# Softmax times V on one core: range checks on the chip and a second, conditional loop

## The chip, the core and the metric

The kernel runs on one core of a Trainium2 chip. The core has five engines with an instruction stream each: TensorE (PE, matrix products; loads of its stationary operand are listed as PEld), VectorE (DVE), ScalarE (ACT), GpSimd (POOL) and SyncE (SP, which here issues every DMA). Names with a q (SPq, PEldq, DVEq) stand for an engine's sequencer: register, branch, semaphore and DMA-issuing instructions, which the profile does not count as busy time. Tiles live in SBUF, results of PE in PSUM. The metric is the device time of the whole program in microseconds; before the change it is 1063.91 us, the median of three runs (1063.54 to 1064.08).

## The reference

Inputs are `scores` of shape 8 x 12 x 1024 x 1024 and `v` of shape 8 x 12 x 1024 x 64, both float32 and normally distributed.

```python
scores_max = np.max(scores, axis=-1, keepdims=True)
attn = np.exp(scores - scores_max)
attn = attn / (np.sum(attn, axis=-1, keepdims=True) + 1e-8)
return np.matmul(attn, v).astype(np.float32)
```

There are 96 heads (8 x 12). Scores are 403 MB, v and the output 25 MB each.

## The kernel before

The kernel takes exp of the scores without subtracting the row maximum, in fp16, and gets each row's sum as an extra column of the product: v is kept in fp16 with columns of ones behind its 64 columns (`vones`, D + 1 = 65 columns used), so that the 65th column of the result is the sum of the row's exponentials.

A loop on the chip (line 307) runs over the heads in steps of AHEAD = 4; one pass of the loop is called a pass here, and there are 24. Within a pass the four heads (k = 0 to 3) and the eight rows of each (r = 0 to 7; a "row" is a block of 128 query rows) are written out. A row goes through these steps:

- ACT takes exp of 128 x 1024 scores from `s_nat` to `p_nat` (line 266), two rows per instruction, single rows in the last head of a pass after its first pair.
- PE turns the row in eight 128 x 128 pieces into PSUM, `psT` (line 279).
- DVE copies `psT` to SBUF, `pt` (line 286).
- PE multiplies the eight pieces of `pt` with `vones` and accumulates 65 columns in a PSUM bank, `psO` (line 150). This runs three rows behind the transposes (LAG = 3); four rows share a bank.
- After four rows, `normalise` has DVE take the reciprocals of the four sums (line 128) into `recip` and multiply (line 134, two instructions) into `out_sb`.

Data is moved in large pieces. Scores come as 4 MB per head into one of four buffers `s_nat0` to `s_nat3` (line 202), v as 1 MB per four heads into the only buffer `v_sb` (line 214); POOL casts v into `vones` with four instructions per head (`spread_v`, line 223) when that head's products are done, for the pass after. The output goes back as 512 KB per two heads (line 175).

The order on SP is fixed by hand (`queue`): in a pass it is scores of head 0, scores of head 1, store of heads 0 and 1, and then, in conditional blocks at the end (`last`, lines 240 and 247), scores of head 2, v, scores of head 3, store of heads 2 and 3. Each is a wait for the buffer and then a DMA; the v load waits until POOL has cast the last head of the pass. The last two passes take other arms of these conditionals: the scores of the very last head come in pieces of 3, 2, 1, 1 and 1 rows, and the last pass loads nothing. The order of PE's instructions is fixed by `in_line`. DVE's order is left to the planner that schedules the loop body, but for the places where `after` pins an instruction behind another. At the end of the loop each engine compares and branches (line 307); at the end of the program SP waits for all that is under way, and the engines meet in three barriers (line 336).

Of the kernel before, what the change touches and what calls it, by code (L numbers as in the profile page):

```python
# [7 lines left out]

FP32 = mybir.dt.float32
FP16 = mybir.dt.float16  # L10
EXP = mybir.ActivationFunctionType.Exp


@with_exitstack
def kernel(
# [6 lines left out]
    nc = tc.nc  # L22
    P = 128

    B, H, SQ, SK = scores.shape
    Bv, Hv, SKv, D = v.shape
    assert (B, H, SK) == (Bv, Hv, SKv)
    BH = B * H
    assert SQ % P == 0 and SK % P == 0
    R = SQ // P  # L30
    C = SK // P
    M = D + 1
    EB = 2
    G = 4
    LAG = 3
    AHEAD = 4
    Q = P // AHEAD
    S = P // Q
    L = 4
    T = 2  # L40

# [3 lines left out]
    sc_bh = scores.rearrange("b h (p r) j -> (b h) p r j", p=P)  # L47
    v_bh = v.rearrange("b h (i t) d -> (b h i) (t d)", i=Q)


    W = P // T
    out_bh = out.rearrange("b h (j x) d -> (b h j) (x d)", j=W)

    const_pool = ctx.enter_context(tc.tile_pool(name="const", bufs=1))
    sb_pool = ctx.enter_context(tc.tile_pool(name="sbpool", bufs=1))
    ps_pool = ctx.enter_context(tc.tile_pool(name="pspool", bufs=1, space=bass.MemoryType.PSUM))

    ident32 = const_pool.tile([P, P], FP32, name="ident32")
    make_identity(nc, ident32)
    order16 = const_pool.tile([P, P], FP16, name="order16")  # L60

    nc.vector.tensor_copy(  # L62
        out=order16[:].rearrange("p (t j) -> p t j", t=T),
        in_=ident32[:].rearrange("p (j t) -> p t j", t=T),
    )


    vones_bufs = []
    for k in range(AHEAD):
        vo = const_pool.tile([P, C, D + 2], FP16, name=f"vones{k}")  # L70
        nc.vector.memset(vo[:, :, D : D + 2], 1.0)  # L71
# [4 lines left out]
    def buffers(pool, count, shape, dtype, name):  # L76
        return [pool.tile(shape, dtype, name=f"{name}{k}") for k in range(count)]

    s_bufs = buffers(sb_pool, AHEAD, [P, R, SK], FP32, "s_nat")
    v_sb = sb_pool.tile([P, C // L, S, L, D], FP32, name="v_sb")  # L80
    p_bufs = buffers(sb_pool, 8, [P, EB, SK], FP16, "p_nat")
    pt_bufs = buffers(sb_pool, 4, [P, SK], FP16, "pt")
    out_bufs = buffers(sb_pool, 2, [P, T, R, D], FP32, "out_sb")
    rc_bufs = buffers(sb_pool, 2, [P, R // G, G, 1], FP32, "recip")
    psT_bufs = buffers(ps_pool, 4, [P, SK], FP16, "psT")


    psO_bufs = buffers(ps_pool, 2 * (R // G), [P, 512], FP32, "psO")
    turn = {}

    def take(bufs):
        k = turn.get(id(bufs), 0)
        turn[id(bufs)] = k + 1
        return bufs[k % len(bufs)]
# [5 lines left out]
    def after(a, b):  # L100

        tc.add_manual_dep(
            a.ins,
            b.ins.name,
            mybir.DependencyInfo(mybir.DependencyClass.NoSync, mybir.DependencyReason.DATA),
            reason="order",
        )

    def in_line(op):

        if line:
            after(op, line[-1])
        line.append(op)

    def queue(dma):

        if queued:
            after(dma, queued[-1])
        queued.append(dma)

    def one(bh, n):
        return bh[bass.ds(n, 1)].rearrange("o p r d -> (o p) r d")

    def normalise(k, st, b, behind=None):

        psO = st["psO"][b][:, 0 : G * M].rearrange("p (g m) -> p g m", m=M)
        recip = st["recip"][:, b]
        inverse = nc.vector.reciprocal(out=recip, in_=psO[:, :, D : D + 1])  # L128
        if behind is not None:
            after(inverse, behind)  # L130
        h = k % T
        for t in range(T):
            part = slice(t * W, (t + 1) * W)
            nc.vector.tensor_tensor(  # L134
                out=st["out_sb"][h * W : (h + 1) * W, t, b * G : (b + 1) * G, :],
                in0=psO[part, :, 0:D],
                in1=recip[part].to_broadcast([W, G, D]),
                op=mybir.AluOpType.mult,
            )

    def finish(u):

        n0, k, r, pt, st = u
        b, g = r // G, r % G
        if r == 0:
            st["recip"] = take(rc_bufs)
            st["out_sb"] = out_bufs[k // T]
        bank = st["psO"][b]
        for c in range(C):
            product = nc.tensor.matmul(  # L150
                out=bank[:, g * M : (g + 1) * M],
                lhsT=pt[:, c * P : (c + 1) * P],
                rhs=st["vones"][:, c, 0:M],
                start=(c == 0),
                stop=(c == C - 1),
            )
            in_line(product)
        if g == G - 1 and (b > 0 or k < AHEAD - 1):
            normalise(k, st, b)
        if r == R - 1:  # L160
            spread_v(k)
            if k == T - 1:
                store(n0, 0)
# [35 lines left out]
    def load(k, n, parts=(R,), r=0, **cond):  # L199
        for rows in parts:  # L200
            queue(
                nc.sync.dma_start(  # L202
                    out=s_bufs[k][:, r : r + rows, :],
                    in_=one(sc_bh, n)[:, r : r + rows, :],
                    **cond,
                )
            )
            r += rows
# [11 lines left out]
    def spread_v(k):  # L220

        for s in range(S):
# [4 lines left out]
                in_=v_sb[k * Q : (k + 1) * Q, :, s],  # L227
            )

    def load_next(k, n0):  # L230

        if k < AHEAD - 2:
            load(k, (n0 + (AHEAD + k)) % BH, cond=n0 < BH - AHEAD)

    def last(n0):


        before = queued[-1:]

        with tc.If(n0 < BH - 2 * AHEAD) as cmp:  # L240
            queued[:] = before
            load(AHEAD - 2, (n0 + (2 * AHEAD - 2)) % BH)
            load_v((n0 + 2 * AHEAD) % BH)
            load(AHEAD - 1, (n0 + (2 * AHEAD - 1)) % BH)
            store(n0, AHEAD - T)
        with cmp.Else():
            with tc.If(n0 < BH - AHEAD) as cmp2:
                queued[:] = before
                load(AHEAD - 2, BH - 2, (4, 4))
                load(AHEAD - 1, BH - 1, (3,))  # L250
                store(n0, AHEAD - T)
                load(AHEAD - 1, BH - 1, (2, 1, 1, 1), 3)
            with cmp2.Else():
                queued[:] = before
                store(n0, AHEAD - T, whole=False)

    def heads(n0):

        for k in range(AHEAD):
            st = dict(vones=vones_bufs[k], psO=[take(psO_bufs) for b in range(R // G)])  # L260
            for r in range(R):
                if r % EB == 0:
                    p_nat = take(p_bufs)
                    rows = 1 if k == AHEAD - 1 and r > 0 else EB
                    for g in range(0, EB, rows):
                        exp = nc.scalar.activation(  # L266
                            out=p_nat[:, g : g + rows, :].rearrange(
                                "p r (x v) -> p x r v", v=Q * L
                            ),
                            in_=s_bufs[k][:, r + g : r + g + rows, :].rearrange(  # L270
                                "p r (i x l) -> p x (r i) l", i=Q, l=L
                            ),
                            func=EXP,
                        )
                        rewrite(p_nat, exp)
                p_row = p_nat[:, r % EB, :].rearrange("p (h q l) -> p h l q", q=P, l=L)
                psT = take(psT_bufs)
                for c in range(C):
                    turned = nc.tensor.transpose(  # L279
                        out=psT[:, c * P : (c + 1) * P],  # L280
                        in_=p_row[:, c // L, c % L, :],
                        identity=order16[:],
                    )
                    in_line(turned)
                pt = take(pt_bufs)
                copy = nc.vector.tensor_copy(out=pt[:], in_=psT[:])  # L286
                rewrite(pt, copy)
                if k == AHEAD - 1 and r == R - 1:

                    normalise(k, st, 0, copy)  # L290
                if r == R - 1:
                    load_next(k, n0)
                pending.append((n0, k, r, pt, st))
                if len(pending) > LAG:
                    finish(pending.pop(0))
        while pending:
            finish(pending.pop(0))
        last(n0)

    assert BH % AHEAD == 0 and BH >= 2 * AHEAD and SK == Q * S * C  # L300
    load_v(0)
    for k in range(AHEAD):
        load(k, k)
    for k in range(AHEAD):
        spread_v(k)
    load_v(AHEAD)
    with tc.For_i(0, BH, AHEAD, iteration_sync="reg_based") as n0:  # L307
        queued.clear()
        line.clear()
        heads(n0)  # L310


# [28 lines left out]
```

## Time and profile before

| | |
|---|---|
| median of three runs | 1063.91 us (1063.54 to 1064.08) |
| span of the profiled execution | 1061.94 us |
| last DVE instruction ends | 1057.94 us |
| last store issued, landed | 1058.36 us, 1060.23 us |
| bytes moved | 453.05 MB, mean 427 GB/s |
| exp, two rows (line 266) | 1901 ns, x312 |
| copy of a turned row (line 286) | 691 ns, x768 |
| reciprocal of 128 x 4 (line 128) | 174 ns, x192 |
| product of 64 x 256 (line 134) | 422 ns, x384 |
| cast of 32 x 512 (line 223) | 607 ns, x400 |

Times of single instructions are from the profile's table of groups; a mean is over all instructions of that line and shape. In a timeline, a line gives start, length, engine, source line, operation and count, and in brackets how long the engine had been idle before it and what ended that idle time. "Landing" of a DMA is when its last bytes are reported.

### The profile page before, as it was taken

How to read it: one execution, taken by the hardware profiler on the slowest of the kernel's cores; microseconds unless marked ns; L12 is line 12 of the kernel's file. 1: busy time of each engine (PE TensorE's matmuls, PEld its weight loads, DVE VectorE, ACT ScalarE, POOL GpSimd, SP SyncE). 2: the span in 40 equal slices, each digit the busy share in tenths (PEclk: the TensorE clock that was granted, in tenths of full speed). 3: DMA queues.
4: the chain of work that ended last, by engine and by line, in shares of the span. 5: the costliest groups of instructions: out<-in, count | busy, mean ns of one | idle time of the engine just before them, and what ended most of it. 6: DMA issues, size and time to landing. Idle time of an engine off the chain costs nothing.

```text
span 1061.9 us, 32592 instructions
## 1 busy us (share of the span) xinstructions
PE 723.4 (68%) x12288; PEld 688.6 (65%) x12288; DVE 702.2 (66%) x1349; ACT 740.1 (70%) x480; POOL 243.5 (23%) x406
## 2 busy tenths in 40 slices
PE   2766766667666777667586676867667676666776
PEld 2756766667666667666576675766566676666765
DVE  1766666757667666666676666766667576676767
ACT  3766776667767668676685866767666677666686
POOL 3122211131121311212112121122111311213113
PEclk9888888878888788887988778888888788898889
DMA  9999999999999999999999999999999999999996
GB/s 395 433 410 435 434 434 433 427 433 431 433 430 433 434 433 436 428 431 429 432 432 434 434 431 434 425 438 430 430 434 432 435 424 440 431 430 434 428 430 271
DMA packets 25332, 453.05 MB, mean 427 GB/s; under 512 B 2801, under 2 KB 3313, under 8 KB 9713
## 3 DMA queue, kind: packets, MB, share of 16 engines
q1 hardware_dynamic: 25328, 453.00, 99.4%
q8 instruction: 3, 0.05, 0.0%
q14 instruction: 1, 0.00, 0.0%
HBM read 436.21 MB, written 25.17 MB: 434 GB/s over the span
## 4 chain that ended last, share of the span: by engine, by line
DMA 61%; PE 14%; ACT 5%; PEld 5%; DVE 4%; POOL 3%; issue 3%; SPq 1%; POOLq 1%; ACTq 0%
DMA s_nat<-in_scores_dram 61%; PE psT L279 8%; PE psO L150 6%; ACT p_nat L266 5%; DVE pt L286 4%; POOL vones L223 3%; PEld L279 3%; PEld L150 2%; SPq L214 1%; SPq L202 0%; POOLq L223 0%; POOLq L240 0%; POOLq L307 0%; POOLq L336 0%; ACTq L266 0%
## 5 line engine op out<-in xcount | busy, mean ns | idle before, releaser
L266 ACT ACTIVATE p_nat<-s_nat 128x2048 f16<-128x2048 f32 (+1 forms) x456 | 709.3, 1630 | 219.1 <-DMA s_nat<-in_scores_dram 191.1
L279 PE MATMUL psT<-order,p_nat 128*128 128x128 f16 x6144 | 573.1, 250 | 314.3 <-ACT p_nat L266 313.8
L286 DVE COPY pt<-psT 128x1024 f16<-128x1024 f16 x768 | 520.4, 691 | 286.8 <-PE L150 102.5
L279 PEld LDWEIGHTS <-p_nat 128*128 128x128 f16 x6144 | 458.4, 125 | 341.3 <-ACT p_nat L266 340.9
L223 POOL CAST vones<-v_sb 32x512 f16<-32x512 f32 x400 | 242.8, 607 | 815.5 <-PE L279 442.8
L150 PE MATMUL psO<-vones,pt 128*128 128x65 f16 x6144 | 357.5, 205 | 18.4 <-DVE pt L286 17.7
L150 PEld LDWEIGHTS <-pt 128*128 128x128 f16 x6144 | 302.1, 107 | 26.0 <-DVE pt L286 25.1
L134 DVE TENSOR_TENSOR out_sb<-psO,recip 64x256 f32<-64x256 f32 x384 | 162.2, 422 | 62.3 <-DMA out_dram<-out_sb 50.3
L266 ACT ACT_TABLE_LOAD x24 | 30.8, 1283 | 94.3 <-PE psO L150 59.5
L128 DVE RECIPROCAL recip<-psO 128x4 f32<-128x4 f32 x192 | 33.4, 174 | 5.5 <-PE psO L150 5.5
L71 DVE MEMSET vones<- 128x16 f16 x4 | 0.2, 72 | 0.8 <-PEq L325 0.8
L62 DVE CAST order<-ident 128x128 f16<-128x128 f32 x1 | 0.2, 226 | 0.4 <-POOL ident masks.py:199 0.4
masks.py:199 POOL TENSOR_SCALAR_AFFINE_SELECT ident<-ident 128x128 f32<-128x128 f32 x1 | 0.3, 292 | 0.1
masks.py:197 POOL MEMSET ident<- 128x128 f32 x1 | 0.2, 204 | 0.3 <-POOLq L325 0.3
L325 POOL MEMSET const-float32-0.0<- 128x1 f32 x1 | 0.1, 98 | 0.3 <-issue 0.3
L325 POOL MEMSET const-bfloat16-1.0<- 128x1 bf16 x1 | 0.1, 100 | 0.0
L325 POOL MEMSET const-uint8-127<- 128x1 uint8 x1 | 0.1, 100 | 0.0
L325 POOL MEMSET const-float32-1.0<- 128x1 f32 x1 | 0.1, 98 | 0.0
## 6 DMA issues: line engine op xcount, KB each, us to landing
s_nat<-in_scores_dram SPq DMA_DIRECT2D x96, 4096.0 KB, 32.5
v_sb<-in_v_dram SPq DMA_DIRECT2D x24, 1024.0 KB, 18.6
out_dram<-out_sb SPq DMA_DIRECT2D x47, 512.0 KB, 26.2
s_nat<-in_scores_dram SPq DMA_DIRECT2D x2, 2048.0 KB, 31.4
s_nat<-in_scores_dram SPq DMA_DIRECT2D x1, 1536.0 KB, 32.2
s_nat<-in_scores_dram SPq DMA_DIRECT2D x3, 512.0 KB, 20.8
s_nat<-in_scores_dram SPq DMA_DIRECT2D x1, 1024.0 KB, 25.0
out_dram<-out_sb SPq DMA_DIRECT2D x1, 256.0 KB, 2.5
```

The source lines that it names most:

```text
L62: nc.vector.tensor_copy(out=order16[:].rearrange("p (t j) -> p t j", t=T), in_=ident32[:].rearrange("p (j t) -> p t j", t=T),)
L71: nc.vector.memset(vo[:, :, D : D + 2], 1.0)
L128: inverse = nc.vector.reciprocal(out=recip, in_=psO[:, :, D : D + 1])
L134: nc.vector.tensor_tensor(out=st["out_sb"][h * W : (h + 1) * W, t, b * G : (b + 1) * G, :], in0=psO[part, :, 0:D], in1=recip[part].to_broa ...
L150: product = nc.tensor.matmul(out=bank[:, g * M : (g + 1) * M], lhsT=pt[:, c * P : (c + 1) * P], rhs=st["vones"][:, c, 0:M], start=(c == 0) ...
L214: nc.sync.dma_start(out=v_sb[:].rearrange("x h s l d -> x (h s l d)"), in_=rows[bass.ds(n // AHEAD, 1)].rearrange("o x y -> (o x) y"),)
L223: nc.gpsimd.tensor_copy(out=vones_bufs[k][s * Q : (s + 1) * Q, :, 0:D].rearrange("i (h l) d -> i h l d", l=L), in_=v_sb[k * Q : (k + 1) * ...
L266: exp = nc.scalar.activation(out=p_nat[:, g : g + rows, :].rearrange("p r (x v) -> p x r v", v=Q * L), in_=s_bufs[k][:, r + g : r + g + ro ...
L279: turned = nc.tensor.transpose(out=psT[:, c * P : (c + 1) * P], in_=p_row[:, c // L, c % L, :], identity=order16[:],)
L286: copy = nc.vector.tensor_copy(out=pt[:], in_=psT[:])
L325: nc = _bacc.Bacc("TRN2", target_bir_lowering=False, num_devices=1)
```

## The change

Three things are added, and one is moved.

The reciprocals of the row sums are no longer written to two small buffers in turn, but to columns of one tile `seen` with 1 + 32 + 1 columns: one column for each of the 32 rows of a pass, one at the left for the smallest value seen so far, one at the right for the largest. At the end of each pass `spread_of(seen, 32)` brings both up to date with two reductions on DVE, and `judge` compares them with limits (sums between 1 and 60000), combines that with the verdict on v, and counts with a 128 x 1 matmul over the partitions how many of the 128 partitions are within the limits. DVE copies the count to an integer.

The sizes of v are watched: in each pass, after rows 3 and 7 of head 2 (k = AHEAD - 2), DVE takes the largest absolute value of two quarters of `v_sb` (128 x 512 each), and after row 7 brings the smallest and the largest of these up to date and compares them with limits (2^-6 to 60000). The same is done once before the loop for the first four heads' v.

After the loop all engines load the count and branch on it. If it is below 128, `general` computes all heads again in fp32 with the row maximum subtracted; the loop of it runs over the 96 heads one by one. The arm that falls through is the one without it.

```diff
-    rc_bufs = buffers(sb_pool, 2, [P, R // G, G, 1], FP32, "recip")
+    seen = const_pool.tile([P, 1 + AHEAD * R + 1], FP32, name="seen")
+    nc.vector.memset(seen, 1.0)
+    v_seen = const_pool.tile([P, 1 + VC + 1], FP32, name="v_seen")
+    nc.vector.memset(v_seen, 1.0)
...
     def normalise(k, st, b, behind=None):
...
-        recip = st["recip"][:, b]
+        at = 1 + k * R + b * G
+        recip = seen[:, at : at + G].rearrange("p (g o) -> p g o", o=1)
...
+    def spread_of(tile, n):
+
+        nc.vector.tensor_reduce(out=tile[:, 0:1], in_=tile[:, 0 : n + 1], axis=X, op=ALU.min)
+        nc.vector.tensor_reduce(
+            out=tile[:, n + 1 : n + 2], in_=tile[:, 1 : n + 2], axis=X, op=ALU.max
+        )
+
+    def watch_v(parts):
+        for i in parts:
+            flat = v_sb[:].rearrange("x h s l d -> x (h s l d)")
+            n = (C // L) * S * L * D // VC
+            nc.vector.tensor_reduce(
+                out=v_seen[:, 1 + i : 2 + i],
+                in_=flat[:, i * n : (i + 1) * n],
+                axis=X,
+                op=ALU.max,
+                apply_absolute_value=True,
+            )
+
+    def within(out, tile, n, low, high, also=None):
+        part = small("part")
+        if also is None:
+            nc.vector.tensor_scalar(
+                out=part, in0=tile[:, n + 1 : n + 2], scalar1=high, scalar2=None, op0=ALU.is_le
+            )
+        else:
+            nc.vector.scalar_tensor_tensor(
+                out=part, in0=tile[:, n + 1 : n + 2], scalar=high, in1=also,
+                op0=ALU.is_le, op1=ALU.mult,
+            )
+        nc.vector.scalar_tensor_tensor(
+            out=out, in0=tile[:, 0:1], scalar=low, in1=part, op0=ALU.is_ge, op1=ALU.mult
+        )
...
+    def judge(bank):
+
+        within(right, seen, AHEAD * R, 1.0 / SUM_MAX, 1.0, also=fits[:])
+        cell = bank[0:1, G * M : G * M + 1]
+        in_line(
+            nc.tensor.matmul(
+                out=cell, lhsT=right[:], rhs=vones_bufs[0][:, 0, D : D + 1], start=True, stop=True
+            )
+        )
+        nc.vector.tensor_copy(out=count[:], in_=cell)
+
+    def general():
+
+        s, x = s_bufs[0], s_bufs[1]
...
+        with tc.For_i(0, BH, 1) as n:
+            nc.sync.dma_start(out=s[:], in_=one(sc_bh, n))
...
+            for r in range(R):
+                nc.vector.tensor_reduce(out=lift, in_=s[:, r, :], axis=X, op=ALU.max, negate=True)
+                nc.scalar.activation(out=p_row, in_=s[:, r, :], func=EXP, bias=lift[:])
...
                 if k == AHEAD - 1 and r == R - 1:
 
                     normalise(k, st, 0, copy)
+                if k == AHEAD - 2 and r % G == G - 1:
+                    watch_v(range(r // G * VC // (R // G), (r // G + 1) * VC // (R // G)))
+                    if r == R - 1:
+                        spread_of(v_seen, VC)
+                        within(fits, v_seen, VC, V_MIN, V_MAX)
...
         while pending:
             finish(pending.pop(0))
+        spread_of(seen, AHEAD * R)
+        judge(st["psO"][-1])
         last(n0)
...
     for k in range(AHEAD):
         load(k, k)
+    watch_v(range(VC))
+    spread_of(v_seen, VC)
     for k in range(AHEAD):
         spread_v(k)
...
         heads(n0)
+
+    good = nc.values_load(count[:], min_val=0, max_val=P)
+    with tc.If(good < P, preferred_fallthrough_block=False):
+        general()
```

## The prediction

> **What bounds the kernel now.** I read the page first (busy shares, then the DMA queue's share), then the waits of the SP queue, then a timeline of one steady pass of the loop, then the last pass, where the steady state ends.
>
> ```profile
> span 1061.9 us, 32592 instructions
> PE 723.4 (68%) x12288; PEld 688.6 (65%) x12288; DVE 702.2 (66%) x1349; ACT 740.1 (70%) x480; POOL 243.5 (23%) x406
> ...
> q1 hardware_dynamic: 25328, 453.00, 99.4%
> ```
>
> No engine is over 70% busy, while the one queue that carries all data is busy for 99.4% of the span: the loop runs at the pace of the DMA. One steady pass (four heads) shows how much room is behind that; ACT's exponentials first, then what SP issues:
>
> ```profile
> 572.82 7.60 ACT L266 ACTIVATE p_nat<-s_nat 128x2048 f16<-128x2048 f32 x7 [4.78 <-DMA s_nat<-in_scores_dram]
> ...
> 604.38 7.31 ACT L266 ACTIVATE p_nat<-s_nat 128x2048 f16<-128x2048 f32 x4 [3.60 <-DMA s_nat<-in_scores_dram]
> 616.51 7.60 ACT L266 ACTIVATE p_nat<-s_nat 128x2048 f16<-128x2048 f32 x7 [4.82 <-DMA s_nat<-in_scores_dram]
> ```
> ```profile
> 570.19 0.34 SPq L202 DMA_DIRECT2D s_nat<-in_scores_dram  x1
> 587.96 0.33 SPq L214 DMA_DIRECT2D v_sb<-in_v_dram  x1
> 588.67 0.33 SPq L202 DMA_DIRECT2D s_nat<-in_scores_dram  x1
> ```
>
> ACT waits for scores; the period is 616.51 - 572.82 = 43.69 us. The latest issue is the pair at 587.96 and 588.67 (v, then head 3's scores), and what was queued ahead of it (the scores issued at 570.19) lands only at 604.38. So the pass can end some 604.4 - 588.7 = 15.7 us later before the DMA runs dry.
>
> The room ends with the last pass, which has no loads behind it. By stretches (start:end, length, busy us of PE, PEld, DVE, ACT, POOL, clock, DMA share), and DVE in order of time:
>
> ```profile
> 1024.70:1033.20 8.50, 7.48 (x119) 7.18 (x118) 6.43 (x11) 7.41 (x5) 0.00 (x0) 0.77 1.00 426
> 1033.20:1054.70 21.50, 18.68 (x374) 17.03 (x371) 19.86 (x39) 19.26 (x14) 7.27 (x12) 1.00 0.84 353
> ```
> ```profile
> 1043.40 0.69 DVE L286 COPY pt<-psT 128x1024 f16<-128x1024 f16 x1 [0.18 <-PE L279]
> 1044.13 0.88 DVE L134 TENSOR_TENSOR out_sb<-psO,recip 64x256 f32<-64x256 f32 x2
> 1045.04 1.94 DVE L286 COPY pt<-psT 128x1024 f16<-128x1024 f16 x3
> 1046.89 0.17 DVE L128 RECIPROCAL recip<-psO 128x4 f32<-128x4 f32 x1
> 1047.24 0.69 DVE L286 COPY pt<-psT 128x1024 f16<-128x1024 f16 x1 [0.18 <-PE L279]
> 1047.96 0.88 DVE L134 TENSOR_TENSOR out_sb<-psO,recip 64x256 f32<-64x256 f32 x2
> 1048.87 1.94 DVE L286 COPY pt<-psT 128x1024 f16<-128x1024 f16 x3
> 1050.73 0.17 DVE L128 RECIPROCAL recip<-psO 128x4 f32<-128x4 f32 x1
> 1051.08 0.69 DVE L286 COPY pt<-psT 128x1024 f16<-128x1024 f16 x1 [0.18 <-PE psT L279]
> 1051.80 0.87 DVE L134 TENSOR_TENSOR out_sb<-psO,recip 64x256 f32<-64x256 f32 x2
> 1052.71 1.94 DVE L286 COPY pt<-psT 128x1024 f16<-128x1024 f16 x3
> 1054.92 0.69 DVE L286 COPY pt<-psT 128x1024 f16<-128x1024 f16 x1 [0.27 <-PE L150]
> ```
>
> In the 21.5 us up to 1054.7 DVE is busy for 19.86 us, with idle bits of 0.18 us: it is the fullest engine, and its copies run 0.6 to 1.3 us behind the transposes that feed them (the last transposes end at 1054.25, their copy starts at 1054.92). Whatever DVE gets to do after 1033 moves the end.
>
> **The sum's base.** The profiled execution has a span of 1061.94 us; the median of the three runs is 1063.91, 1.97 us more, which I carry over. The measurement tells about 0.2% (2.1 us) from no change.
>
> **The change, part by part.**
>
> The reads of v (four reductions of 128x512 in head 2, after rows 3 and 7). No row has a reduction. The 128x4 reciprocal takes 174 ns and the 64x256 product 422 ns, 0.98 ns per element more; 512 elements come to 0.67 us. Bounds: 0.35 us, if it goes at the 0.65 us per 1024 of the f16 copies, and 0.69 us, a copy's whole time. I take 0.67 (it is f32, as the product is): 2.7 us a pass. Minimum, maximum and two comparisons of a few elements follow, each waiting for the one before: four times 0.174 + 0.035 (the gap from reciprocal to product at 1055.7), 0.84 us. Together 3.5 us of DVE per pass.
>
> In 23 passes that costs nothing: the cover is the 15.7 us. v lands in time, because it is queued right behind the scores of head 2: those land at 604.38, POOL's first cast of the new v starts at 606.89, and DVE copies row 3 of that head at 611.30. The v load now waits for DVE too, but it already waits for POOL's last cast of the pass, 10 us after head 2. Behind that wait on SP stand head 3's scores and a store, which is why the 15.7 us count.
>
> In the last pass the 3.5 us fall at 1044 and 1048, where DVE is behind. Of the idle bits after that (0.18, 0.18, 0.27) about 0.4 us can be filled. Cost 3.1 us. Bounds: 1.4 + 0.84 - 0.6 = 1.6 us and 2.8 + 0.84 = 3.6 us where the code's place holds; nothing, if the work comes where DVE idles (a rival).
>
> The judging at the end of each pass (minimum and maximum over 33 columns, two comparisons, a matmul, a copy to an integer). DVE needs about 4 x 0.21 = 0.85 us before PE may start, and PE's matmul stands ahead of the next pass's first transposes. In steady passes it is covered as above. At 1023 us, into the last pass, DVE's last product ends at 1023.0 and PE starts the new transposes at 1023.73; with the judging they start at about 1024.2. From there the chain has no wait for a load that takes it up: 0.45 us, from 0 to 0.8. After the last pass, judging takes 0.85 + 0.3 + 0.2 = 1.4 us from DVE's end at 1057.94, while the last store, issued at 1058.36, lands at 1060.23, and SP waits for that: nothing, with 0.9 us to spare.
>
> The branch at the end. All five engines load the count into a register, compare, branch, and meet again. I read the first of the closing barriers (1060.50 to 1060.93) as the loop's own, so this lies behind it, uncovered. Comparing and branching: the compare-branches take 0.05 to 0.23 us, SP's corrections of semaphores in an arm not taken five steps from 1058.75 to 1059.28; 0.4 us. The load has no row. From below, a register move, 0.03 us; from above, the smallest store's 2.0 us from issue to landing. I take the table load's 1.28 us, the only row in which an engine fetches something for itself from memory. Together 1.7 us, from 0.1 to 2.8. The Trainium skill, DMA: Bandwidth & Descriptors, Latency and other measured facts, gives about 0.6 us as a floor for such a load; by it the part is an estimated 1.0 us, and no trace here shows it.
>
> The rest costs nothing: the first v check (4 reductions at 5.7 us) lies in DVE's idle time until 21.2 us; two memsets of 0.07 us are at the start, 20 us before DVE's first copy; the reciprocals are only written elsewhere, by the same engine.
>
> Sum: 3.1 + 0.45 + 1.7 = 5.3 us. 1061.94 + 5.3 + 1.97 = **1069.2 us**, 0.5% slower; its own range 1066 to 1072 from the bounds.
>
> **The rivals.**
>
> *DVE takes it in; not slower.* If the reductions stand where DVE is free (before the last pass's first copy it idles 1.80 us, then 0.16 to 0.60 us a row until 1033), or if the loads (the last row lands at 1052.28) and ACT (its last row starts at 1052.51) set the end instead, only the branch is left: 1063.9 + 1.7 = 1065.6, within 0.2%. It decides from under 0.4 us for DVE's part in the last pass. For it: ACT and the loads end within a microsecond of DVE. Against it: 3.5 us against idle bits of 0.6 us. Chance 0.20, of which 0.06 ends just over the bound and 0.02 below the old time by 0.2%.
>
> *The reads come too early.* DVE's order in the trace isn't the code's: the memsets of line 71 run at 0.82 us, ahead of the cast of line 62 (1.35 us) that the code has first, and a copy stands between each reciprocal and its products. Nothing in a pass holds the reads of v back, so they may stand ahead of the first copy, and DVE then waits in each pass until v lands (20 us into it). In the first pass DVE starts at about 46.5 us; 32 rows at 0.96 us and the casts bring v's next load to 81 or 82 us, some 5 us after the queue's last bytes (76.8). Later passes just hold the period, but the pass before the last ends about 9 us late, less 1.8 us of idle. 1063.9 + 5 + 7 + 1.7 = 1078. Against it: SP's loads are paced by DMA, and a plan that knows that puts the reads late. Chance 0.14.
>
> *The skip stalls on code.* If the way past the second loop is a jump over its code, the engines wait for instructions. The trace has three fetches of 16 KB, 0.88 to 0.96 us each, in the first pass, and none at the jump back; PE's compare-branch there takes 0.22 us and its next instruction follows within 0.06 us. With a fetch of 1 us and a landing of 2 us: 1069.2 + 3 = 1072. Chance 0.10. The Trainium skill, Runtime: NRT & Kernel Launch, Instruction fetch mechanics, says that a taken branch to a page outside the two held ones forces such a fetch; by it the time would be that 1072, and the trace's jump back, which has a prefetch hint ahead of it, doesn't show the stall.
>
> That the second loop runs would add at least 96 loads of 9.6 us, over 900 us; sums of 1024 exponentials of normal values lie near 1700, far inside the limits. I give it nothing.
>
> **How the numbers follow.** Forecast 0.56, taken in 0.20, too early 0.14, stall 0.10. Slower: 0.56 + 0.06 + 0.14 + 0.10 = 0.86; within 0.2%: 0.12; faster: 0.02. The range reaches from the taken-in case's 1065 (leaving out its lower part, some 0.05) to 1075 (leaving out the early reads, 0.14).
>
> **What would show it.** Period still 43.7 us and queue share near 99%; DVE busy near 702 + 24 x 4.4 = 808 us; reductions at about 0.67 us, standing in head 2 or 3; in the last pass DVE's final copy about 3.5 us after 1054.92 with the last load still landing near 1052; from the last store's landing to the end about 1.7 + 1.7 us. The prediction is wrong if DVE waits for v in a pass, if the last copy comes no later, or if the registers take several microseconds.

## The result, and the profile after

The changed kernel takes 1117.77 us (median of four runs, 1116.0 to 1121.26), the kernel before 1063.74 us beside it: a ratio of 1.0512, with a 95% interval from 1.0494 to 1.0531. That is 54.0 us slower, where 5.3 us were predicted, and outside the range of 1065 to 1075 us.

The page of the changed kernel, the lines that answer to the first fence of the prediction (busy us, share of the span, instructions; then packets, MB and share of the queue):

```profile
span 1114.9 us, 33161 instructions
...
PE 737.6 (66%) x12312; PEld 704.0 (63%) x12312; DVE 781.5 (70%) x1669; ACT 745.2 (67%) x480; POOL 243.8 (22%) x406
...
q1 hardware_dynamic: 25328, 453.00, 96.5%
```

DVE has 79 us more work (the prediction had 106), and at 70% is still no fuller than ACT was before. But the queue is at 96.5% instead of 99.4%: something lets it run dry. The page's 40 slices of the span show where (busy tenths of the DMA, first before, then after):

```profile
DMA  9999999999999999999999999999999999999996
DMA  9979999999999999999999999999999999999971
```

It runs dry between the first pass and the second and again at the end, but not in the passes between. By the packet records the queue is idle for 39 us in place of 6, and busy for 20 us longer. The table of waits names what holds it up (engine and line, what it waited for: us in total, times, longest):

```profile
PE psO L166 <- DVE pt L403: 270.4, 215, 27.1
...
DVE v_seen L257 <- DMA v_sb<-in_v_dram: 225.1, 24, 38.6
...
DVE v_seen L257 <- DMA s_nat<-in_scores_dram: 6.2, 1, 6.2
```

Line 257 is the reduction over v. In 24 places, one of them ahead of the loop, DVE stands still until a v load has landed, 225 us in all, and PE then waits for DVE's copies for 270 us. The timeline of DVE shows where in the pass that is: a steady pass first, then the last one (start, length, line, operation, count, and the idle time before it):

```profile
533.97 2.47 DVE L257 TENSOR_REDUCE v_seen<-v_sb 128x1 f32<-128x512 f32 x4 [8.08 <-DMA v_sb<-in_v_dram]
536.48 0.16 DVE L248 TENSOR_REDUCE v_seen<-v_seen 128x1 f32<-128x5 f32 x1
...
537.00 3.07 DVE L403 COPY pt<-psT 128x1024 f16<-128x1024 f16 x5
...
1071.60 2.46 DVE L257 TENSOR_REDUCE v_seen<-v_sb 128x1 f32<-128x512 f32 x4 [6.24 <-DMA s_nat<-in_scores_dram]
...
1074.62 3.07 DVE L403 COPY pt<-psT 128x1024 f16<-128x1024 f16 x5
...
1103.23 0.69 DVE L403 COPY pt<-psT 128x1024 f16<-128x1024 f16 x1 [0.27 <-PE L166]
```

All four reductions stand together, ahead of the first copy of the pass, and not in head 2 where the code has them. DVE can start a pass only when v has come. In the last pass no v is loaded, but DVE still waits there, until 1071.60 us: the releaser named is a load of scores. It is the second half of head 2's, which tells of its landing (1071.47) by the semaphore that v's load uses in the other passes, and the reductions wait for that semaphore. From then on its 32 copies run one behind the other (28.6 us from 1074.62 to 1103.23).

SP's queue in two neighbouring passes:

```profile
526.28 0.33 SPq L230 DMA_DIRECT2D v_sb<-in_v_dram  x1
527.00 0.33 SPq L218 DMA_DIRECT2D s_nat<-in_scores_dram  x1
...
529.81 1.19 SPq L218 DMA_DIRECT2D s_nat<-in_scores_dram  x2
556.24 0.36 SPq L191 DMA_DIRECT2D out_dram<-out_sb  x1
557.15 0.34 SPq L218 DMA_DIRECT2D s_nat<-in_scores_dram  x1
570.95 0.33 SPq L230 DMA_DIRECT2D v_sb<-in_v_dram  x1
```

Before, a v load landed 18.6 us after its issue (median), because other transfers were queued ahead; now it is 7.7 us. After 529.81 nothing is issued for 26 us. And the distance from one v load to the next is 44.67 us, 1.0 us over the old period. Two stretches of one pass each, an early and a late one, give (length, busy us of PE, PEld, DVE, ACT, POOL, granted clock, DMA share, GB/s), first before, then after:

```profile
234.40:278.00 43.60, 30.78 (x512) 29.61 (x512) 28.97 (x57) 30.82 (x20) 9.71 (x16) 0.80 1.01 433
627.40:671.10 43.70, 30.44 (x512) 29.11 (x512) 28.67 (x56) 30.88 (x21) 9.71 (x16) 0.80 1.00 432
```
```profile
242.50:286.70 44.20, 30.48 (x515) 29.08 (x514) 32.40 (x69) 31.07 (x21) 9.66 (x17) 0.81 1.00 428
645.60:690.80 45.20, 31.03 (x526) 29.63 (x525) 32.99 (x71) 31.04 (x21) 10.26 (x18) 0.81 1.00 422
```

The DMA share is 1.00 or 1.01 in all four, but the rate falls from 433 to 428 and 422 GB/s: the packets themselves take longer.

At the end of the program, the rows of the branch (duration min/median/max in ns, first and last start; line 439 is the branch, line 438 the load of the count):

```profile
L439 SPq COMPARE_BRANCH  x2: 46/48/49, 1109.9 to 1110.5; - x2
...
L439 PEldq COMPARE_BRANCH  x2: 74/1872/3670, 1110.0 to 1110.3; - x2
```
```profile
L438 DVEq TENSOR_LOAD <-count x1: 558/558/558, 1109.4 to 1109.4; - x1
...
L438 SPq FUSED_REGOPS  x1: 181/181/181, 1113.3 to 1113.3; - x1
```

The loads take 0.48 to 0.56 us. PE's second compare-branch takes 3.67 us, and SP, which branched at 1110.5, does its next thing at 1113.3.

With these, the 53.0 us between the two profiled executions (1114.92 less 1061.94) can be laid out by time. ACT's table load opens each pass: the second pass starts 7.4 us late (65.5 against 58.1 us), the last pass 30.2 us late (1050.64 against 1020.47). From there to the last copy it takes 52.6 us against 34.5 (18.1 more), and from the last copy to the end 11.7 us against 7.0 (4.7 more).

### The profile page after: what moved, and what is told of

The parts are those of the page before. It is cut to its first block, busy times and chain, and to the rows that moved or that the text cites. A ratio compares the mean times of both kernels' runs of the same rounds, so it can differ in the third digit from the quotient of the medians.

```text
span 1114.9 us, 33161 instructions
## 1 busy us (share of the span) xinstructions
PE 737.6 (66%) x12312; PEld 704.0 (63%) x12312; DVE 781.5 (70%) x1669; ACT 745.2 (67%) x480; POOL 243.8 (22%) x406
## 3 DMA queue, kind: packets, MB, share of 16 engines
q1 hardware_dynamic: 25328, 453.00, 96.5%
## 4 chain that ended last, share of the span: by engine, by line
PEld 41%; DMA 20%; DVE 17%; PE 10%; issue 5%; POOL 3%; POOLq 1%; PEldq 0%; SPq 0%; DVEq 0%
PEld L396 21%; PEld L166 20%; DMA v_sb<-in_v_dram 18%; DVE pt L403 12%; PE psO L166 6%; PE psT L396 5%; DVE v_seen L257 4%; POOL vones L239 3%; DMA s_nat<-in_scores_dram 2%; DVE part L268 0%; POOLq L239 0%; DVE v_seen L249 0%; POOLq L357 0%; PEldq L166 0%; DVE out_sb L151 0%
## 5 line engine op out<-in xcount | busy, mean ns | idle before, releaser
L166 PE MATMUL psO<-vones,pt 128*128 128x65 f16 x6144 | 389.1, 199 | 270.5 <-DVE pt L403 270.4
L396 PE MATMUL psT<-order,p_nat 128*128 128x128 f16 x6144 | 537.2, 240 | 30.2 <-ACT p_nat L383 21.2
L403 DVE COPY pt<-psT 128x1024 f16<-128x1024 f16 x768 | 503.8, 688 | 66.2 <-PE L396 23.3
L166 PEld LDWEIGHTS <-pt 128*128 128x128 f16 x6144 | 319.7, 101 | 299.3 <-issue 242.7
L396 PEld LDWEIGHTS <-p_nat 128*128 128x128 f16 x6144 | 446.7, 120 | 31.9 <-ACT p_nat L383 25.0
L257 DVE TENSOR_REDUCE v_seen<-v_sb 128x1 f32<-128x512 f32 x100 | 61.6, 678 | 231.3 <-DMA v_sb<-in_v_dram 225.1
L151 DVE TENSOR_TENSOR out_sb<-psO,seen 64x256 f32<-64x256 f32 x384 | 161.8, 421 | 11.3
L145 DVE RECIPROCAL seen<-psO 128x4 f32<-128x4 f32 x192 | 33.7, 176 | 5.5 <-PE psO L166 5.5
L276 DVE SCALAR_TENSOR_TENSOR right<-seen,part 128x1 f16<-128x1 f32 x24 | 11.1, 462 | 0.8
L248 DVE TENSOR_REDUCE seen<-seen 128x1 f32<-128x33 f32 x24 | 4.5, 188 | 0.8
L249 DVE TENSOR_REDUCE seen<-seen 128x1 f32<-128x33 f32 x24 | 4.2, 177 | 0.0
```

The costliest lines, as they stand in the source:

```text
L151: nc.vector.tensor_tensor(out=st["out_sb"][h * W : (h + 1) * W, t, b * G : (b + 1) * G, :], in0=psO[part, :, 0:D], in1=recip[part].to_broa ...
L166: product = nc.tensor.matmul(out=bank[:, g * M : (g + 1) * M], lhsT=pt[:, c * P : (c + 1) * P], rhs=st["vones"][:, c, 0:M], start=(c == 0) ...
L248: nc.vector.tensor_reduce(out=tile[:, 0:1], in_=tile[:, 0 : n + 1], axis=X, op=ALU.min)
L249: nc.vector.tensor_reduce(out=tile[:, n + 1 : n + 2], in_=tile[:, 1 : n + 2], axis=X, op=ALU.max)
L257: nc.vector.tensor_reduce(out=v_seen[:, 1 + i : 2 + i], in_=flat[:, i * n : (i + 1) * n], axis=X, op=ALU.max, apply_absolute_value=True,)
L276: nc.vector.scalar_tensor_tensor(out=out, in0=tile[:, 0:1], scalar=low, in1=part, op0=ALU.is_ge, op1=ALU.mult)
```

## The experiments

Two theories stood at first. *Order*: the planner's place for the reads makes DVE wait for v, and that is nearly all. *Work*: more work on DVE per pass is what costs. Once the first four runs were in, two more came up for what was left, *addresses* and *code*.

**Reads pinned behind their rows.** Each reduction is tied behind the copy of the row after which the code has it.

```diff
-    def watch_v(parts):
+    def watch_v(parts, behind=None):
...
+            if behind is not None:
+                after(largest, behind)
...
-                    watch_v(range(r // G * VC // (R // G), (r // G + 1) * VC // (R // G)))
+                    watch_v(range(r // G * VC // (R // G), (r // G + 1) * VC // (R // G)), copy)
```

> All work of the change stays; each reduction of v is pinned behind the copy of the row where the code has it, so DVE no longer stands still for v at the front of a pass. Order theory (DVE waits for v in each pass, and v's load, the 32 rows and the casts become one loop that is longer than the DMA's 43.7 us): period back at 43.7 us, and what is left is 3.1 us for the reductions in the last pass, 0.45 us for the judging and the 4.7 us that the changed kernel's trace shows between the last store's landing and the end: 1063.7 + 8.3 = 1072 us. Work theory (4.4 us more of DVE per pass make its chain too long wherever they stand): 1105 us or more.

Measured: 1076.29 us (1075.74 to 1076.48), ratio 1.0117 (1.0100 to 1.0133). With all of the work kept, 41.5 of the 54 us are gone. It is 4 us above what the order theory gave: the last pass starts 5.1 us late, which the theory did not have. The 4.7 us at the end, which it had taken from the changed kernel's trace, are there again (4.8). Both are taken up below.

**No reads of v in the loop**, and **the same work with nothing to wait for**.

```diff
-                if k == AHEAD - 2 and r % G == G - 1:
-                    watch_v(range(r // G * VC // (R // G), (r // G + 1) * VC // (R // G)))
-                    if r == R - 1:
-                        spread_of(v_seen, VC)
-                        within(fits, v_seen, VC, V_MIN, V_MAX)
...
+    within(fits, v_seen, VC, V_MIN, V_MAX)   # once, before the loop
```
```diff
+    still = const_pool.tile([P, (C // L) * S * L * D], FP32, name="still")
+    nc.vector.memset(still, 1.0)
...
-            flat = v_sb[:].rearrange("x h s l d -> x (h s l d)")
+            flat = still[:]
```

> Leaves out the check of v in the loop (the check before the loop stays, so v of heads 4 to 95 is unchecked); sums, judging, branch and second loop stay. Both theories: 1063.7 + 0.45 + 4.7 = 1069 us; the difference to the pinned kernel is the price of the reductions in the last pass, 3.1 us by the prediction's sum.

> The four reductions stay at the front of each pass, with the same sizes, but read a constant tile instead of v, so there is nothing to wait for (the check of v is left out thereby). Order theory: period 43.7 us; in the last pass 3 us of reductions stand before the first copy, where DVE had 1.8 us idle: 1063.7 + 0.45 + 1.3 + 4.7 = 1070 us. Work theory: as slow as the changed kernel, 1110 us or more.

Measured: 1074.20 us (1073.26 to 1074.20) without the reads, 1073.89 us (1073.19 to 1074.20) with the same reductions of a tile that is always there. Four reductions at the front of each pass cost nothing that shows as long as they wait for nothing: the work theory falls. Both are 4 to 5 us above the expectation, in the same way as the pinned kernel: their period is 43.77 us at first and 44.0 us from about the middle on.

**The wait alone**: one small reduction per pass in place of four.

```diff
-                    watch_v(range(r // G * VC // (R // G), (r // G + 1) * VC // (R // G)))
+                    watch_v(range(1 if r < G else 0), 1)    # first run: 1 element
+                    watch_v(range(1 if r < G else 0), 8)    # second run: 8 elements
```

The second argument is new: how many elements of each partition the reduction reads.

> One reduction of a single element of v per partition in place of four of 512, at the front of the pass as in the changed kernel: the wait stays, 2.3 us of work per pass go (the check of v covers one element of each partition). Order theory: the loop from v's load to the next is 2.3 us shorter than the 44.2 to 45.3 us of the changed kernel and so hides under the DMA's 43.7 us, but each pass still starts its rows only when v is there, and the last pass only when the second half of head 2's scores is there (both use one semaphore), 1040 us in the kernel before; 32 rows from there end some 16 us later than before: 1063.7 + 16 + 4.7 = 1085 us. Work theory: 1070 us.

> The changed kernel with the reads of v cut to one reduction of 8 elements in each partition, at the front of each pass where it can only go once v has landed: this leaves out nearly all of the check of v, and some 2.3 us of DVE work a pass, and keeps the wait. Waiting theory: DVE still stands until v lands in every pass, the last pass starts only with the second half of the scores of head 2 in the pass before; time 1085 to 1117 us, the nearer to 1117 the less the work itself counts. Work theory: near 1074 us, as the kernel with no reads.

The first gave 7452 us, and its time says nothing on the wait: a single value in each of 128 partitions is not enough to stay above 2^-6, the kernel's own limit, in every pass, so the second loop ran. The trace gives its price: from the load of the count at 1101 us to the end at 7448 us, 6347 us or 66 us a head. With 8 elements it is 1108.03 us (1104.48 to 1108.72), and the table of waits has the same line as the changed kernel:

```profile
DVE v_seen L257 <- DMA v_sb<-in_v_dram: 266.6, 24, 38.5
```

So the wait alone, with 2.3 us of the work per pass left out, makes 33.8 of the 43.6 us that lie between the kernel without reads (1074.20) and the changed one (1117.77). I put the rest to the reductions themselves, which at this place delay all that DVE does after its wait. No run separates that further; between the two traces, 2.7 us of it lie in the first pass, 4.1 us between the second pass and the last, and 1.8 us in the last.

**Addresses.** The small new tiles lie in front of the large ones in SBUF. `s_nat0` starts at byte 21504 of a partition before (84 x 256) and at 21920 after, 160 past a multiple of 256. Two kernels shift the kernel before, by a tile that nothing reads; one puts the pinned kernel back on a multiple of 256.

```diff
+    gap = const_pool.tile([P, 40], FP32, name="gap")   # before + 160 bytes; 32: + 128 bytes; 24, pinned: + 96
+    nc.vector.memset(gap, 0.0)
```

> The kernel before with one more constant tile of 160 bytes per partition that nothing reads. It moves every tile behind it in SBUF by 160 bytes, so that the scores' buffers start 160 bytes past a multiple of 256, as they do in the three pinned or unread runs before. Address theory (the longer period of those runs, 43.8 to 44.0 us against 43.67 us, comes from where the transfers land): the pass starts fall behind by 4.7 to 5 us until the last pass, time near 1068.5 us. Rival (it comes from the added instructions, or from their semaphores): 1063.7 us, period 43.67 us.

> The first pinned kernel (1076.3 us) with a constant tile of 96 bytes per partition that nothing reads, so that the scores' buffers start at a multiple of 256 bytes again. Address theory: the 4.7 to 5 us of the period go, time near 1071.4 us, packets of 32 KB back at 1213 ns. Rival (the added work lengthens the period): 1076.3 us.

> The kernel before with a constant tile of 128 bytes per partition that nothing reads: the scores' buffers start 128 bytes past a multiple of 256. If what counts is a multiple of 256 bytes: period 43.77 to 44.0 us and near 1068.8 us, as with 160 bytes. If a multiple of 128 or 64 is enough: 1063.8 us, period 43.67 us.

Measured: 1068.85 us (1068.70 to 1068.97; ratio 1.0047, 1.0031 to 1.0064) for the kernel before with 160 bytes, 1068.58 us with 128 bytes (1.0044, 1.0028 to 1.0061), and 1071.03 us (1070.52 to 1071.32; ratio 1.0067, 1.0050 to 1.0083) for the aligned pinned kernel. A shift alone costs 5.0 us, and taking it out of the pinned kernel gives 5.3 us back; 128 bytes are not enough. ACT's table loads in the kernel shifted by 160 bytes give a period of 44.02 us:

```profile
629.48 1.28 ACT L268 ACT_TABLE_LOAD   x1 [3.34 <-PE psO L152]
...
673.50 1.28 ACT L268 ACT_TABLE_LOAD   x1 [3.33 <-PE psO L152]
```

So the shift is the cause. The trace's records of packets and landings show two things that come with it. First, on a multiple of 256, all but 0.7% of the 32 KB packets take 1213 ns. Shifted by 160 bytes, 43% take longer, half of these by 1 to 3 ns and the rest mostly by 4 to 17 ns (median 1221 ns); shifted by 128 bytes it is 36%, and the longer ones are at a median of 1218 ns. The mean packet is 1.8 ns longer, 0.15%. With 32 such packets a pass on each of the 16 DMA engines, and 8 of 8 KB that are 3 ns longer, that comes to an estimated 0.08 us a pass; the period is 0.09 us longer from the start (43.77 us). Second, from about the middle of the loop one of the sixteen parts of each load falls behind. The other fifteen go on landing within 2.5 us of each other, all sixteen land within 2.4 us early on and within 6.0 us at the end, 0.24 us more with every pass, and the period is longer by another 0.24 us (44.0 us). The longer packets are far more than the one in sixteen that belong to that part, so they alone don't tell why it falls behind, and why only from the middle on; that stays open. The Trainium skill, DMA: Bandwidth & Descriptors, How a descriptor splits into AXI transactions, says that a read which doesn't start on a multiple of 256 bytes is begun at the boundary below, and that the bytes in front still cost beats of 32 bytes. If that held for the written side, which is the one shifted here, 160 bytes would be 5 beats on 1024, an estimated 6 ns, and 128 bytes 5 ns. The longer packets show 1 to 17 ns, which is of that order, but the page speaks of reading, and no run shows that this is the reason.

In the aligned pinned kernel the last pass starts at 1020.3 us (before: 1020.5), and two stretches of one pass are as before:

```profile
234.20:277.80 43.60, 30.58 (x513) 29.31 (x513) 32.52 (x70) 30.83 (x20) 9.79 (x16) 0.80 1.01 432
627.20:670.90 43.70, 30.16 (x513) 28.84 (x513) 32.26 (x69) 30.87 (x21) 9.78 (x16) 0.80 1.00 432
```

So the steady passes take 3.6 us of added DVE work for nothing, as predicted, once the reads stand in head 2. In its last pass the work stands where the prediction put it:

```profile
1045.04 1.28 DVE L259 TENSOR_REDUCE v_seen<-v_sb 128x1 f32<-128x512 f32 x2
1046.35 1.89 DVE L407 COPY pt<-psT 128x1024 f16<-128x1024 f16 x3
...
1049.72 1.28 DVE L259 TENSOR_REDUCE v_seen<-v_sb 128x1 f32<-128x512 f32 x2
...
1054.88 2.48 DVE L407 COPY pt<-psT 128x1024 f16<-128x1024 f16 x4
```

Its last copy starts at 1056.68 us, 1.76 us later than before.

**Code.** The pinned and aligned kernel with the body of the second loop cut to one of eight row blocks, and then with the second loop replaced by one load. (Without the second loop two small tiles go, so the constant tile there is 160 bytes in place of 96; the buffers start at the same multiple of 256.)

```diff
-            for r in range(R):
+            for r in range(1):
```
```diff
     def general():
+        nc.sync.dma_start(out=s_bufs[0][:], in_=one(sc_bh, 0))
-        ...
```

> The pinned and aligned kernel, with the second loop's body cut to one of its eight row blocks: this leaves out seven eighths of the second loop's work, which is skipped on these values, so only the length of the code that is jumped over changes. Code theory (the last branch waits for instructions from beyond that code): the end gets shorter, by up to 2.8 us against the aligned kernel with the full loop, to near 1068.5 us by address theory. Rival (the wait is for the load of the register, or for the meeting of the engines, or a jump over even the short code needs the same fetch): no change, 1071.4 us.

> The pinned and aligned kernel (1071.0 us) with the second loop replaced by one load: this leaves out the whole fallback computation, which is skipped on these values; the load of the count, the comparison and the branch stay. Code theory: the three engines that stood still behind the branch (PE 4.8 us, DVE 4.1 us and SP 3.9 us in the aligned kernel, DVE 3.1 us and SP 2.7 us with a body of one eighth) go on at once, the end gets 2.5 to 4 us shorter, time 1067 to 1068.5 us. Rival (they wait for something else, such as the fetch of the closing instructions behind any branch): 1070.5 to 1071 us.

Measured: 1070.90 us (1070.14 to 1071.04) with the short body, 1067.15 us (1066.85 to 1067.72; ratio 1.0032, 1.0019 to 1.0045) without the second loop. The rows of the branch, PE's with the full body first, then in the kernel with the short body:

```profile
L443 PEldq COMPARE_BRANCH  x2: 83/2446/4809, 1063.4 to 1063.9; - x2
```
```profile
L443 SPq COMPARE_BRANCH  x2: 46/48/49, 1064.2 to 1064.9; - x2
...
L443 PEldq COMPARE_BRANCH  x2: 83/203/323, 1064.4 to 1064.6; - x2
```
```profile
L442 SPq FUSED_REGOPS  x1: 181/181/181, 1067.6 to 1067.6; - x1
```

and without the second loop:

```profile
L398 SPq COMPARE_BRANCH  x2: 46/48/49, 1063.4 to 1063.6; - x2
...
L398 PEldq COMPARE_BRANCH  x2: 83/202/320, 1063.6 to 1063.7; - x2
```
```profile
L397 SPq FUSED_REGOPS  x1: 181/181/181, 1063.8 to 1063.8; - x1
```

PE's compare-branch takes 4.81 us with the full body and 0.32 us where PE has only an eighth of the code to get past. SP, whose code the short body leaves as long as it was, still goes on only 2.7 us after its branch, and DVE 3.0 us after its own, though its row blocks are an eighth too. So the code theory's forecast for the short body, near 1068.5 us, missed: the engines meet only when the last is there. The way from the last copy to the end is 11.6 us, and in the kernels with the full body it is 11.6 to 12.9 us, so nothing that can be told is gained. Without the second loop SP and DVE go on at once, the way is 8.5 us, and 3.9 us are gone. The stall belongs to the code that is jumped over; what decides how long each engine stands is not shown.

The DMA table lists fetches of instructions apart from the program's data (packets, MB, share of the queue), for one of the two queues that carry them first before, then after the change:

```profile
q14 instruction: 1, 0.00, 0.0%
```
```profile
q14 instruction: 4, 0.03, 0.0%
```

These four are packets of 8 KB, and all lie behind the branch: they start from 1111.2 to 1114.0 us, beside one of 16 KB on the other queue at 1111.25 us. The kernel before fetches nothing after 47.6 us. With the short body the four of 8 KB and one of 16 KB are there as well; without the second loop none of 8 KB is, and one of 16 KB at 1065.1 us, when the engines have gone on. The records don't say for which engine a packet is. The Trainium skill, Runtime: NRT & Kernel Launch, Instruction fetch mechanics, names such a fetch at a branch to code that isn't held; these runs agree and give it a price of 3.9 us.

**What makes the period of the changed kernel longer.** The changed kernel as it is, but aligned; and then with the v load queued ahead of head 2's scores.

```diff
+    gap = const_pool.tile([P, 24], FP32, name="gap")
+    nc.vector.memset(gap, 0.0)
...
-            load(AHEAD - 2, (n0 + (2 * AHEAD - 2)) % BH)
             load_v((n0 + 2 * AHEAD) % BH)
+            load(AHEAD - 2, (n0 + (2 * AHEAD - 2)) % BH)   # second run only
```

> The changed kernel as it is, reads of v at the front of each pass, with a constant tile of 96 bytes per partition that nothing reads, so that the scores' buffers start at a multiple of 256 bytes. Loop theory (in the changed kernel the chain load of v, reads, 32 rows, casts, next load of v sets the period, not the transfers): only part of the 5 us goes, the period stays above 43.9 us, time 1108 to 1116 us. Rival (the early reads cost a fixed delay and the longer period is the addresses' alone): period 43.67 us, time 1117.8 less 5 or more, 1095 to 1108 us.

> The kernel of the run before this one, with the load of v queued ahead of the scores of head 2 instead of behind them. Loop theory: v lands some 4 us earlier after its issue, the chain falls under the period of the transfers, the period returns to 43.67 us and the delay stops growing over the passes: some 10 to 20 us less than the run before. Rival (what counts is only that DVE waits, not what the load stands behind): within 3 us of the run before.

Measured: 1112.37 us (1112.32 to 1112.77), then 1111.98 us (1111.84 to 1112.24). Aligning gives 5.4 us, as it does elsewhere. Loading v first gives nothing in the sum (0.4 us, where the loop theory had 10 to 20). But this is no clean test of the theory. v lands 7.4 us after its issue in place of 7.7, so the 4 us that the run was to bring did not come; and the order has a price of its own, because head 2's scores now stand behind v's wait for the casts: the second pass takes 54.4 us in place of 44.7. The passes after it, up to the last, are 4.2 us shorter together, and the last is 5.5 us shorter up to its last copy. Late in the loop a pass still takes about 45 us in both. So the theory that the chain from v load over reads, rows and casts to the next v load sets the period is not borne out, and for the early passes not ruled out either. An early and a late pass of the aligned kernel show where the time goes late in the loop:

```profile
241.90:285.90 44.00, 31.13 (x518) 29.80 (x517) 32.44 (x69) 31.10 (x21) 9.83 (x17) 0.81 1.01 434
641.40:686.40 45.00, 30.35 (x504) 28.95 (x502) 31.74 (x68) 31.09 (x21) 9.02 (x16) 0.77 1.00 422
```

The DMA is busy throughout, at a lower rate late in the loop. The packet records have 6% of the 32 KB packets of the second half of the loop above 1.26 us, up to 2.75 us, where the kernel before and the aligned pinned kernel have none. Four fifths of them start within 3 us of the moment when a store's packets begin to move, nearly always at the same one of a pass's two stores. This comes with the early reads and goes with them; what in the DMA or the memory makes these packets slow stays open.

**The sum.** The 54.0 us, step by step from the changed kernel to the kernel before. The steps follow on each other, so that they add up is no test; the figures in brackets are, where the same step was taken from another kernel:

| cause | difference | us |
|---|---|---|
| place of the reads | 1112.37 - 1071.03, aligned (unaligned 1117.77 - 1076.29 = 41.5) | 41.3 |
| addresses | 1117.77 - 1112.37 (pinned 5.3, kernel before 5.0) | 5.4 |
| code of the second loop | 1071.03 - 1067.15 | 3.9 |
| the rest: checks, load of the count, branch | 1067.15 - 1063.76 | 3.4 |
| together | measured: 54.0 | 54.0 |

The changed kernel's own time is known to some 2 us, so the 5.4 us is no surer than that; the two figures beside it come from kernels with less spread.

The best kernel with the whole function is the pinned and aligned one, 1071.03 us: 46.7 us faster than the changed kernel, and 0.7% above the kernel without checks.

## Why the prediction was wrong

*The bound.* Right: the queue at 433 GB/s sets the period, and there is room behind it in each pass. The aligned pinned kernel keeps 43.67 us with 3.6 us more DVE work per pass. That the room is some 15 us no run measures.

*The reads of v: the step that failed.* "In 23 passes that costs nothing: the cover is the 15.7 us" holds for the place that the code gives them, which the prediction took over. The trace has them ahead of the first copy in every pass, and there DVE's first copy comes 26.4 us into a pass (537.0, pass start 510.6) where it came 4.3 us into it before (631.7, pass start 627.4): 22 us later, more than the cover. The delay is not paid anew in each pass: though DVE starts 22 us late, one pass follows the other after 43.8 to 45.6 us, and the wait itself shows in the first pass (7.4 us) and the last (18.1). In all this place of the reads costs 41.3 us where the prediction had nothing. The prediction had the evidence (DVE's order in the trace of before is not the code's, and nothing holds the reads back) and put it into a rival, "The reads come too early", at a chance of 0.14, on the argument that a planner which knows that the loads are paced by the DMA would put the reads late. It did not.

*That rival's own sum, 1078 us,* has the mechanism right and three sizes wrong. The bubble of the first pass was put at 5 us and is 7.4. "Later passes just hold the period" is wrong: another 22.8 us come between the start of the second pass and that of the last, 4.8 of them by the addresses (980.4 us in the aligned kernel instead of 985.2), most of the rest late in the loop, where the slow packets are. And the last pass was put at 7 us and costs 18.1: the rival carried a delay over from the pass before and had nothing for DVE to wait for in the last pass, but it waits there too, for a load of scores, until 21 us into the pass.

*The size of a reduction.* 0.67 us was taken; each takes 0.678 us by its own row, and 0.62 us in a group of four that overlap a little (2.47 us). Right.

*The last pass, 3.1 + 0.45 us.* Measured on the kernels for which this step was meant, the pinned aligned ones: the last copy comes 1.8, 1.9 and 2.7 us later. That is nearer the lower bound of 1.6 us: DVE filled more of its idle time than I had allowed. From the pass's start to the last copy it idles 6.0 us before and 4.6 us in the first of these kernels, 1.4 us filled where I had 0.4. In the run without reads the time from the last pass's start to the last copy is 0.3 us longer, which is the judging.

*The branch, 1.7 us.* In the kernel without a second loop the way from the last copy to the end is 1.4 us longer than before. The load of the count was mis-sized, 0.48 to 0.57 us against the 1.28 us that I took from the table load's row. No trace here shows that the table load fetches from memory, so that row was no ground for it; the lower figure that the prediction cited beside it was the nearer, and the loads came out under it. That the sum is only 0.3 us off is luck: what else lies there (compare, branch, meeting and the last judging) took about 0.9 us instead of 0.4. Nor do the bounds follow from the rows named: 0.4 and the store's 2.0 us make 2.4, not 2.8, and the bounds of the three parts give 1065.6 to 1071.1 us, not 1066 to 1072.

*"The skip stalls on code", 0.10.* This came true as well: rivals need not exclude each other. Its 3 us are 3.9 us.

*Nothing in the prediction asked where the new tiles would lie.* "The rest costs nothing" covered two memsets and a few columns, and overlooked that 416 bytes more per partition move every buffer behind them off a multiple of 256. That is 5 us, as much as my whole forecast.

By its own terms the forecast's parts come to 3.4 us, measured in the kernel without the second loop, against 5.3 predicted; what was missing was 50.6 us in three places outside of them.

## What to carry to other kernels

Where a planner orders an engine's instructions, the place in the code is no place in time. Here an added read of a loaded buffer was put at the front of the pass, and everything that was placed behind it on DVE waited for that load; so look at the order before costing such a read, and pin it behind the work that it should follow. After adding small tiles, look whether the big DMA targets still start on a multiple of 256 bytes; here a pad of 96 bytes was worth 5 us. A fallback that is never run can still cost when it is jumped over: 3.9 us here for a written-out loop body.

## What was not expected of the hardware

- A start 128 or 160 bytes off a multiple of 256 made 36 to 43% of the 32 KB packets 1 to 17 ns longer (1213 ns before); 8 KB packets went from 309 ns to a mean of about 312 ns. The mean 32 KB packet was 0.15% slower, and the kernel 0.45%: from the middle of the loop one part in sixteen of the loads fell behind by 0.24 us a pass. Why one is open.
- With early reads 5 to 6% of the 32 KB packets in the second half of the loop took 1.26 to 2.75 us, mostly around the start of a store, at full DMA share; the rate fell from 433 to 422 GB/s. Why is open.
- A jump over unused code held PE for 3.4 to 4.8 us in the changed kernel and seven of its variants, and SP and DVE for 2.6 to 4.1 us, while ACT and POOL went on at once.
- A load of one register from SBUF took 0.48 to 0.57 us on each of the five engines.
